# Attention scores as 64-row products on alternating halves of the array, in place of DMA-stacked 128-row products

## The chip, the cores and the metric

The kernel runs on one core of a Trainium2 chip. The metric is the device time of one execution in microseconds, the median of several runs. A profile is the record of one execution, taken by the hardware profiler; its times are counted from the first instruction (the span's start).

The names of the engines in the profile: PE is TensorE (matrix products), PEld the loading of its stationary operand, DVE is VectorE, ACT is ScalarE, POOL is GpSimd, and SP is SyncE, which here only issues DMA transfers.

## The reference, cut to what matters

A two-layer encoder over 512 tokens of width 1024: stick-breaking attention with 16 heads of 64, a squared-ReLU MLP of width 4096, a gated linear recurrence, a second MLP, and a final norm. All in float32. The part that the change touches is the score product `z` in

```python
z = jnp.einsum('bhqd,bhkd->bhqk', qb, kb).astype(jnp.float32) * scale   # per 128-query block
mask = k_pos < q_pos
log_keep = jnp.where(mask, jax.nn.log_sigmoid(-z), 0.0)
after = lax.cumsum(log_keep, axis=3, reverse=True) - log_keep
w = jnp.where(mask, jnp.exp(jax.nn.log_sigmoid(z) + after), 0.0)
outs.append(jnp.einsum('bhqk,bhkd->bhqd', w.astype(vb.dtype), vb))
```

Each head contracts over 64 numbers, and each block of 128 queries sees only the keys up to its own end.

## The kernel before, in words

**Precision.** A float32 matrix is split into a high part (rounded to the type fp32r, which PE takes in one pass) and a low part (the rest, again as fp32r). A product of two such matrices is the sum of three products: high by high, high by low, low by high. `three` (lines 234 to 236) does this for the dense layers.

**Attention.** Heads are worked in eight pairs, since two heads of 64 fill the 128 partitions of a tile. For each pair a dense product gives q (128 x 512, head 0 in partitions 0 to 63, head 1 in 64 to 127) and another gives k. ACT copies the product to the high part (line 349), DVE subtracts for the low part (line 350). Then `stacked` (line 341; line 368 for the first pair) issues DMA transfers on SP's queue that rebuild, for each head j, tiles of 128 partitions: `q{j}` holds q's high half above q's low half, `kh{j}` holds k's high half twice, `kl{j}` k's low half twice. That is twelve transfers of 64 x 512 numbers for a pair.

**Scores.** `score_steps` is a generator with eight steps a pair: head by head, and in each head the four query blocks. A step takes one PSUM bank of the tag `z` (there are two) and makes two products over all 128 rows: the stacked q block by `kh` (line 587) and by `kl` (line 588), with max(256, keys) columns, that is 256, 256, 384 and 512. Together they hold all four partial products, low by low too. What follows a step: two sigmoids on ACT (`w`, line 595, and `keep`, line 596, which read the bank; in the first pair DVE first copies the bank out, scaled, in line 593), a mask and a product on POOL (lines 600 and 610), and a scan on DVE (line 606).

**Values.** `value_steps` transposes the weights on PE (line 628), splits them on ACT and DVE, and multiplies by v (lines 654 and 655).

**What sets the order.** PE's order is written by hand: a loop runs over "fill" steps (the dense products of the next pairs' q and k in lines 234 to 236, of v in lines 503 to 505, and of the output projection), and between them it puts the score and value steps by due times: a pair's chain of `n` score steps starts at `SCORE0 + PACE * p` and is spread over `SCORES` = 19 fill steps; the value chain starts 23 fill steps later. The orders of ACT, DVE, POOL and SP are set by a scheduler from the program's dependences. SP's queue carries both the weight slabs (line 221) and the stacking transfers, in one order.

Of the kernel before, what the change touches and what calls it, by code (L numbers as in the profile page):

```python
# [11 lines left out]
F32 = mybir.dt.float32  # L12
BF16 = mybir.dt.bfloat16
F32R = mybir.dt.float32r
AF = mybir.ActivationFunctionType
ALU = mybir.AluOpType
PSUM = bass.MemoryType.PSUM

P = 128
S = 512  # L20
# [18 lines left out]
PACE = 23.7  # L39
SCORE0, SCORES = 12, 19  # L40
# [5 lines left out]
LATER = 1  # L46
# [14 lines left out]
EARLY = 5  # L61
# [3 lines left out]
def hybrid_encoder(  # L65
# [23 lines left out]
    nc = tc.nc  # L89
    V, A, G, PE = nc.vector, nc.scalar, nc.gpsimd, nc.tensor  # L90
# [10 lines left out]
    def bank(tag=None):  # L101
        if tag is None:
            tag = TAGS[turn[0] % len(TAGS)]
            turn[0] += 1
        return psum.tile([P, S], F32, tag=tag, name=f"ps_{tag}")

    def f(ap):
        return ap.bitcast(F32)
# [185 lines left out]
    NB = S // P  # L294
    PAIRS = H // 2
    half = [slice(0, HD), slice(HD, P)]
    so, early = {}, {}

    home = ctx.enter_context(tc.tile_pool(name="home", bufs=1))
    HOMES = (*(("keep", 4),) * 4, *(("w3", 3),) * 3, ("osum", 1))  # L300

    def home_tile(tag, n, name):
        return home.tile([P, S], F32, tag=tag, name=name, bufs=n)

    with ExitStack() as actx:
        hp = actx.enter_context(tc.tile_pool(name="hp", bufs=2))
# [3 lines left out]
        later = sp.tile([P, S], F32, tag="later", name="later")  # L310
# [3 lines left out]
            fill=1.0, base=0, channel_multiplier=1,  # L314
# [3 lines left out]
        for i in range(2):  # L318
            both = []
            for nm in ("h", "l"):  # L320
                t = sp.tile([P, 2 * P], F32R, tag=f"last{nm}{i}", name=f"last{nm}{i}")
# [4 lines left out]
        scans = []  # L326
        for i in range(3):
            sc = sp.tile([P, S + 1], F32, tag=f"scan{i}", name=f"scan{i}")
            G.memset(sc[:, S : S + 1], 1.0)
            scans.append(sc)  # L330

        q, kh, kl, v, w = {}, {}, {}, {}, {}
        norm = {}

        def stacked(tag, parts):

            both = []
            for j in range(2):
                t = hp.tile([P, S], F32R, tag=f"{tag}{j}", name=f"{tag}{j}")
                for a, part in zip(half, parts):  # L340
                    nc.sync.dma_start(out=f(t[a, :]), in_=f(part[half[j], :]))
                both.append(t)
            return both

        def parted(x, tag):

            xh = hp.tile([P, S], F32R, tag=f"{tag}h", name=f"{tag}h", bufs=1)
            xl = hp.tile([P, S], F32R, tag=f"{tag}l", name=f"{tag}l", bufs=1)
            A.copy(xh, x)
            V.tensor_tensor(xl, x, f(xh), ALU.subtract)  # L350
            return xh, xl

        def q_halves(pair, ps):
            q[pair] = stacked("q", parted(ps, "x"))

        def first_halves(pq, pk):

            qh, ql = parted(pq, "x")
            h = hp.tile([P, S], F32R, tag="th", name="th", bufs=3)
            l = hp.tile([P, S], F32R, tag="tl", name="tl", bufs=3)  # L360
            A.copy(h, pk)
            V.tensor_tensor(l, pk, f(h), ALU.subtract)
            q[0], kh[0], kl[0] = [], [], []
            for j in range(2):
                for tag, two, to in (("q", (qh, ql), q), ("kh", (h, h), kh), ("kl", (l, l), kl)):
                    t = hp.tile([P, S], F32R, tag=f"{tag}{j}", name=f"{tag}{j}")
                    for a, part in zip(half, two):
                        nc.sync.dma_start(out=f(t[a, :]), in_=f(part[half[j], :]))
                    to[0].append(t)

        def k_halves(pair, ps):
            ks = hp.tile([P, S], F32, tag="ks", name="ks", bufs=1)
            V.tensor_tensor(ks, ps, norm["r"], ALU.mult)
            h, l = parted(ks, "x")
            kh[pair] = stacked("kh", (h, h))
            kl[pair] = stacked("kl", (l, l))

        def xg_step(ps, k, wh, wl):
            three(ps, xgh[:, k, :], xgl[:, k, :], wh[:, k, :], wl[:, k, :], k == 0, k == C - 1)
# [20 lines left out]
        parts = [slab_parts(w_qk[i, 0], (0, 2, 4, 6, 8)) for i in range(2)]  # L400
# [162 lines left out]
        def late_slab(c, k0, tags):  # L563

            raw = wpool.tile([P, C, P], F32, tag="raw", name="raw", bufs=3)
            nc.sync.dma_start(out=raw[:, k0:, :], in_=w_so[c][:, k0:, :])
            n = (C - k0 + 3) // 4
            tiles = [hp.tile([P, S], F32R, tag=t, name=t) for t in tags]
            for i in range(n):
                a, b = k0 + 4 * i, min(k0 + 4 * i + 4, C)  # L570
                h, l = (t[:, : (b - a) * P].rearrange("p (k f) -> p k f", f=P) for t in tiles[i::n])
                A.copy(h, raw[:, a:b, :])
                V.tensor_tensor(l, raw[:, a:b, :], f(h), ALU.subtract)
            late[c] = Spread(tiles[:n], k0), Spread(tiles[n:], k0)

        late, marks = {}, {}
        turns = [0]

        def score_steps(pair):

            for j in range(2):
                for qb in range(NB):
                    n = (qb + 1) * P
                    nn = max(n, 2 * P)
                    lhsT = q[pair][j][:, qb * P : n]
                    z = bank("z")
                    PE.matmul(z[:, :nn], lhsT, kh[pair][j][:, :nn], start=True, stop=False)
                    PE.matmul(z[:, :nn], lhsT, kl[pair][j][:, :nn], start=False, stop=True)
                    keep = home_tile("keep", 4, "keep")
                    pool = home if qb == NB - 1 else hp  # L590
                    wt = pool.tile([P, n], F32, tag=f"w{qb}", name=f"w{qb}", bufs=3)
                    if pair == 0:
                        V.tensor_tensor(keep[:, :n], z[:, :n], norm["r"][:, :n], ALU.mult)
                        z = keep
                    A.activation(wt, z[:, :n], AF.Sigmoid, scale=norm["rp"][:, qb : qb + 1])
                    marks["keep"] = A.activation(  # L596
                        keep[:, :n], z[:, :n], AF.Sigmoid, scale=norm["rn"][:, qb : qb + 1]
                    )
                    t = wt[:, qb * P : n]
                    G.affine_select(  # L600
                        t, t, pattern=[[-1, P]], compare_op=ALU.is_gt,
                        fill=0.0, base=0, channel_multiplier=1,
                    )
                    sc = scans[turns[0] % 3]
                    turns[0] += 1
                    V.tensor_tensor_scan(  # L606
                        sc[:, S - n : S][:, ::-1], keep[:, :n][:, ::-1], later[:, S - n :][:, ::-1],
                        1.0, ALU.mult, ALU.max,
                    )
                    G.tensor_tensor(wt, wt, sc[:, S - n + 1 : S + 1], ALU.mult)  # L610
                    w[pair, j, qb] = wt
                    yield

        lows = []

# [68 lines left out]
        fill = []  # L684
# [28 lines left out]
        for p in range(PAIRS):  # L713
            less = LESS * (p == PAIRS - 1)
            chains += [
                [score_steps(p), 8, SCORE0 + PACE * p + LATER * (p == 0), SCORES - less - LATER * (p == 0)],
                [value_steps(p), 18, VAL0 + PACE * p + HOLD * (p == 0), VALS - less],
            ]
        inv = inverse()
# [6 lines left out]
        done = 0  # L726
        for i in range(AHEAD, n_fill):
            if i == LATE - 14:
                late_slab(4, EARLY, ("kh0", "kl0"))
                late_slab(5, EARLY, ("kh1", "kl1"))  # L730
            if i == LATE - 8:
                late_slab(6, 0, ("q0", "q1", "kh0", "kh1"))
            if i == LATE:
                x = [home_tile(tag, n, "x") for tag, n in HOMES[:7]]
                for c in range(7):
                    nc.sync.dma_start(out=x[c], in_=xT[:, c, :])
                for c in early:
                    G.tensor_tensor(x[c], x[c], early[c], ALU.add)
            next(steps)
            if i in (SUMS, BROAD):  # L740
                next(inv)
            if i == BROAD:
                with tc.issue_after(norm["copy"].ins):
                    q_halves(*held_halves.pop())
            if i == LATE // 2:
                soft.send(marks["keep"])
            while done < len(due) and due[done][0] < i + 1:
                next(chains[due[done][1]][0])
                done += 1
# [49 lines left out]
    class Mlp:  # L799
# [60 lines left out]
        def square(self, t):  # L860
            self.squares = self.A.activation(t, t, AF.Square)
# [585 lines left out]
    with ExitStack() as rctx:  # L1447
# [35 lines left out]
        ps, xc, aa, a0, om, z, gin, pg = ({} for _ in range(8))  # L1483
        r = None
# [31 lines left out]
        turns = count()  # L1516
# [128 lines left out]
        for k in range(C):  # L1645
            for c in range(4):
                ps, wh, wl = begun[c]
# [195 lines left out]
```

## Time and profile before

| | |
|---|---|
| median of 3 runs | 1028.99 us (1027.84 to 1029.25) |
| the profiled execution | 1029.37 us, span 1027.5 us |
| PE busy | 1019.4 us (99% of the span) |
| DVE, ACT, POOL busy | 857.0, 700.8, 171.1 us |
| score products (lines 587 and 588) | 64 each, first at 28.6 us, last at 205.0 us |
| stacking transfers (lines 341 and 368) | 96 of 128 KB, issued from about 21 to 183 us |

The span is 1.87 us shorter than the profiled execution's own time; sums are made against the latter. A PE record is longer than the time until the next product starts: products are pipelined, and the end of a record is modelled. So what a product costs PE is read from the distance of starts, not from its duration.

### The profile page before, as it was taken

Reading aid. Unit: us, or ns where it says so; the run is one execution under the profiler, and the core shown is the slowest. Engines: PE = TensorE matmul, PEld = TensorE weight load, DVE = VectorE, ACT = ScalarE, POOL = GpSimd, SP = SyncE. Lnnn points to the kernel's source line nnn. Section 1 sums busy time; section 2 is a strip of 40 time slices with the busy share of each in tenths; the row PEclk is TensorE's granted clock in tenths of the full one; section 3 lists DMA queues with packets and bytes.
Section 4 is the critical chain, followed back from the end, with each engine's and each line's share of the span. In section 5 each row is a group of like instructions: output and inputs, shape, how many; then the busy total and the mean of one; then the engine's idle time right before and its main releaser. Section 6 shows DMA issues by size and latency. Waiting matters only on the chain.

```text
span 1027.5 us, 15928 instructions
## 1 busy us (share of the span) xinstructions
PE 1019.4 (99%) x5890; PEld 892.0 (87%) x5890; DVE 857.0 (83%) x1149; ACT 700.8 (68%) x1084; POOL 171.1 (17%) x237
## 2 busy tenths in 40 slices
PE   9999999999999999999999999999999999999997
PEld 7888888888888988988988888888888988988986
DVE  7988787848789898898899888984689898898898
ACT  7777676836766773873875799964755774874866
POOL 0454344420010010010011121200010110010012
PEclk9999999999999999999999999999999999999999
DMA  7745354527537667667682575452436677667653
GB/s 235 222 121 146 120 149 102 160 95 291 136 77 197 170 154 197 172 145 201 176 209 80 152 184 157 103 205 90 97 81 185 166 162 191 166 157 195 170 116 115
DMA packets 53116, 160.46 MB, mean 156 GB/s; under 512 B 6704, under 2 KB 7984, under 8 KB 53040
## 3 DMA queue, kind: packets, MB, share of 16 engines
q1 hardware_dynamic: 41952, 120.21, 35.8%
q0 software_dynamic: 10656, 38.80, 22.9%
q8 instruction: 46, 0.75, 0.3%
q10 hardware_dynamic: 432, 0.44, 0.1%
q14 instruction: 30, 0.25, 0.1%
HBM read 137.41 MB, written 4.19 MB: 138 GB/s over the span
## 4 chain that ended last, share of the span: by engine, by line
PE 90%; DVE 4%; ACT 4%; issue 1%; DMA 1%; SPq 0%; POOL 0%; DVEq 0%; ACTq 0%; POOLq 0%
PE ps_t L1135 15%; PE ps_acc L1000 9%; PE ps_acc L1135 8%; PE ps_z L1000 6%; PE ps_acc L236 5%; PE ps_acc L235 5%; PE ps_acc L234 5%; PE ps_z L1135 4%; PE ps_o L1000 3%; PE ps_t L234 2%; PE ps_t L235 2%; PE ps_t L236 2%; PE ps_o L234 2%; PE ps_o L235 2%; PE ps_o L236 2%; PE ps_z L236 2%
## 5 line engine op out<-in xcount | busy, mean ns | idle before, releaser
L789 ACT CAST wh<-b 128x1024 fp32r<-128x1024 f32 x168 | 174.0, 1051 | 116.9 <-DVE b L789 71.8
L789 DVE TENSOR_TENSOR wl<-b,wh 128x1024 fp32r<-128x1024 f32 x168 | 203.1, 1220 | 37.8 <-ACT wh L789 36.6
L1076 POOL DMA_DIRECT2D b<-in_w_dn x40 | 34.9, 874 | 364.6 <-DVE b L789 268.4
L234 PE MATMUL ps_acc<-xgh,wh 128*128 128x512 f32 x192 | 78.6, 409 | 0.0
L236 PE MATMUL ps_acc<-xgl,wh 128*128 128x512 f32 x192 | 75.3, 392 | 0.0
L235 PE MATMUL ps_acc<-xgh,wl 128*128 128x512 f32 x192 | 75.2, 392 | 0.0
L229 DVE TENSOR_TENSOR wl<-raw,wh 128x512 fp32r<-128x512 f32 (+2 forms) x70 | 62.0, 913 | 15.4 <-ACT wh L227 15.3
L789 ACT ACTIVATE u<-u 128x512 f32<-128x512 f32 x100 | 63.2, 633 | 14.2 <-DVE u L789 12.6
L606 DVE TENSOR_TENSOR_SCAN scan<-keep,later 128x128 f32<-128x128 f32 (+1 forms) x64 | 58.4, 915 | 16.7 <-ACT keep L596 10.4
L227 ACT CAST wh<-raw 128x512 fp32r<-128x512 f32 (+2 forms) x70 | 50.7, 759 | 21.1 <-PE ps_acc L236 7.3
L610 POOL TENSOR_TENSOR w<-w,scan 128x128 f32<-128x128 f32 (+1 forms) x64 | 52.8, 826 | 56.0 <-DVE scan L606 51.3
L789 DVE TENSOR_TENSOR b<-b,b 128x1024 f32<-128x1024 f32 x48 | 58.7, 1223 | 1.2
L1076 POOL DMA_DIRECT2D b<-in_w_up x24 | 20.8, 868 | 231.0 <-DVE b L789 81.1
L789 DVE TENSOR_TENSOR u<-u 128x512 f32<-128x512 f32 (+1 forms) x92 | 54.9, 597 | 4.5 <-ACT u L789 2.5
L789 ACT CAST wh<-raw 128x1024 fp32r<-128x1024 f32 x46 | 48.1, 1048 | 2.5 <-PE ps_acc L1135 2.4
L1135 PE MATMUL ps_t<-wh,bh 128*128 128x512 f32 x120 | 47.0, 392 | 0.1
L1135 PE MATMUL ps_t<-wh,bl 128*128 128x512 f32 x120 | 46.9, 391 | 0.0
L789 DVE TENSOR_TENSOR sl<-u,sh 128x512 fp32r<-128x512 f32 (+2 forms) x50 | 37.5, 750 | 10.3 <-ACT sh L789 10.3
L1000 PE MATMUL ps_z<-xgh,wh 128*128 128x256 f32 x192 | 45.0, 278 | 0.2
L789 DVE TENSOR_TENSOR wl<-raw,wh 128x1024 fp32r<-128x1024 f32 x36 | 44.3, 1231 | 0.8 <-ACT wh L789 0.8
L1000 PE MATMUL ps_acc<-low,wh 128*128 128x256 f32 x192 | 44.7, 277 | 0.0
L789 DVE TENSOR_TENSOR bl<-u,bh 128x1024 fp32r<-128x1024 f32 (+2 forms) x26 | 33.9, 1304 | 12.4 <-ACT bh L789 12.3
(418 smaller groups left out, 3218.1 us busy)
## 6 DMA issues: line engine op xcount, KB each, us to landing
b<-in_w_dn SPq DMA_DIRECT2D x48, 512.0 KB, 4.5
b<-in_w_dn POOLq DMA_DIRECT2D x40, 512.0 KB, 5.8
b<-in_w_up SPq DMA_DIRECT2D x36, 512.0 KB, 4.8
b<-in_w_up POOLq DMA_DIRECT2D x24, 512.0 KB, 5.5
raw<-in_w_m SPq DMA_DIRECT2D x16, 512.0 KB, 4.0
raw<-in_w_dn SPq DMA_DIRECT2D x16, 512.0 KB, 4.6
raw<-in_w_in SPq DMA_DIRECT2D x16, 512.0 KB, 4.0
raw<-in_w_qk SPq DMA_DIRECT2D x12, 512.0 KB, 3.7
```

The source lines that it names most:

```text
L227: A.copy(wh[:, k, :], raw[:, k, :])
L229: V.tensor_tensor(wl[:, k, :], raw[:, k, :], f(wh[:, k, :]), ALU.subtract)
L234: PE.matmul(ps, wh, ah, start=start, stop=False)
L235: PE.matmul(ps, wl, ah, start=False, stop=False)
L236: PE.matmul(ps, wh, al, start=False, stop=stop)
L606: V.tensor_tensor_scan(sc[:, S - n : S][:, ::-1], keep[:, :n][:, ::-1], later[:, S - n :][:, ::-1], 1.0, ALU.mult, ALU.max,)
L610: G.tensor_tensor(wt, wt, sc[:, S - n + 1 : S + 1], ALU.mult)
L789: ins = getattr(self.e, name)(*args, **kwargs)
L1000: PE.matmul(ps[:, i * HS : (i + 1) * HS], m, y, start=new and i == k == low == 0 and y is h, stop=(low, i, k) == steps[-1], skip_group_che ...
L1076: G.dma_start(out=unit[b].rearrange("p j n -> p (j n)"), in_=unit["src"](to), accum_op=ALU.add)
L1135: PE.matmul(sums[to][i], a[:, j, block, i * P : (i + 1) * P], y[:, j, :], start=new and g == j == n == 0 and a is h, stop=g == j == 1 and ...
```

## The change

The stacking is left out. q and k stay as ACT and DVE write them: four tiles `qh`, `ql`, `kh`, `kl` of 128 partitions with the two heads of the pair one above the other. A head's product takes its 64 partitions of both operands. The score generator now has four steps a pair, one for each query block. A step takes both banks of the tag `z`, one for each head, and makes six products of 64 rows: high by high for head 0, for head 1, then q high by k low for both, then q low by k high for both. So consecutive products use different halves of the array's rows and different banks. The low-by-low product is no longer computed. The work after a product (`square`) is the same, for head 0 and then head 1. The due times get `NB` = 4 in place of 8 for the number of steps; the late weight slabs take the new tiles' buffers.

```diff
-        def stacked(tag, parts):
-            both = []
-            for j in range(2):
-                t = hp.tile([P, S], F32R, tag=f"{tag}{j}", name=f"{tag}{j}")
-                for a, part in zip(half, parts):
-                    nc.sync.dma_start(out=f(t[a, :]), in_=f(part[half[j], :]))
-                both.append(t)
-            return both
...
+        def parted(to, pair, tag, x):
+            h, l = (hp.tile([P, S], F32R, tag=f"{tag}{i}", name=f"{tag}{i}") for i in "hl")
+            A.copy(h, x)
+            V.tensor_tensor(l, x, f(h), ALU.subtract)
+            to[pair] = h, l
...
-            for j in range(2):
-                for qb in range(NB):
-                    lhsT = q[pair][j][:, qb * P : n]
-                    z = bank("z")
-                    PE.matmul(z[:, :nn], lhsT, kh[pair][j][:, :nn], start=True, stop=False)
-                    PE.matmul(z[:, :nn], lhsT, kl[pair][j][:, :nn], start=False, stop=True)
...
+            (qh, ql), (kh, kl) = q[pair], ks[pair]
+            for qb in range(NB):
+                n = (qb + 1) * P
+                nn = max(n, 2 * P)
+                zs = [bank("z") for _ in range(2)]
+                for i, (a, b) in enumerate(((qh, kh), (qh, kl), (ql, kh))):
+                    for z, rows in zip(zs, half):
+                        PE.matmul(
+                            z[:, :nn], a[rows, qb * P : n], b[rows, :nn], start=i == 0, stop=i == 2
+                        )
+                for j, z in enumerate(zs):
+                    square(j, qb, n, z)
+                yield
...
-                [score_steps(p), 8, SCORE0 + PACE * p + LATER * (p == 0), SCORES - less - LATER * (p == 0)],
+                [score_steps(p), NB, SCORE0 + PACE * p + LATER * (p == 0), SCORES - less - LATER * (p == 0)],
...
-                late_slab(4, EARLY, ("kh0", "kl0"))
-                late_slab(5, EARLY, ("kh1", "kl1"))
+                late_slab(4, EARLY, ("kh", "kl"))
+                late_slab(5, EARLY, ("kh", "kl"))
...
-                late_slab(6, 0, ("q0", "q1", "kh0", "kh1"))
+                late_slab(6, 0, ("qh", "qh", "ql", "ql"))
```

How this moves the instructions, at the two places of which the prediction speaks. First PE, from the second pair's scores on (names: `ps_z` the score bank, `ps_acc` the running dense product, `w_...` a weight tile that is transposed, `ident` the identity). Before, pair 1's third and fourth block of head 0:

```order
L587 MATMUL ps_z<-kh_736,q_849 128x384
L588 MATMUL ps_z<-kl_742,q_849 128x384
L628 MATMUL ps_t<-ident,w_799 128x128
L234 MATMUL ps_acc<-xgh,wh 128x512
L235 MATMUL ps_acc<-xgh,wl 128x512
L236 MATMUL ps_acc<-xgl,wh 128x512
```

and in the changed kernel, pair 1's first block of both heads:

```order
L236 MATMUL ps_acc<-xgl,wh 128x512
L590 MATMUL ps_z<-kh,qh 128x256 x2
L590 MATMUL ps_z<-kl,qh 128x256 x2
L590 MATMUL ps_z<-kh,ql 128x256 x2
L611 MATMUL ps_t<-ident,w_739 128x128
```

Two products of 128 rows in a step have become six of 64 rows (each row "x2" is one for each half), between neighbours of 128 rows; the steps are half as many.

Second DVE, in the first pair's scores (`keep` from `ps_z` is the copy that frees a bank, `scan_...` the scan's output, `v_...` a value tile). Before:

```order
L593 TENSOR_TENSOR keep<-ps_z,r 128x256
L606 SCALAR_TENSOR_TENSOR scan_118<-keep,later 128x128
L593 TENSOR_TENSOR keep<-ps_z,r 128x384
L350 TENSOR_TENSOR xl<-ks,xh 128x512
L606 SCALAR_TENSOR_TENSOR scan_120<-keep,later 128x256
L593 TENSOR_TENSOR keep<-ps_z,r 128x512
```

and in the changed kernel:

```order
L563 TENSOR_TENSOR keep<-ps_z,r 128x256 x2
L339 TENSOR_TENSOR kl<-ks,kh 128x512
L487 SCALAR_TENSOR_TENSOR v_505<-ps_acc,rc,v_505 128x4x64
L576 SCALAR_TENSOR_TENSOR scan_122<-keep,later 128x256
L576 SCALAR_TENSOR_TENSOR scan_118<-keep,later 128x256
L563 TENSOR_TENSOR keep<-ps_z,r 128x384 x2
```

The copies out of the banks now come in twos, and the third block's copies stand behind both scans of the second block.

More of the change, by code (lines that the diff above doesn't have):

```diff
@@ L330, in hybrid_encoder @@
             scans.append(sc)
-        q, kh, kl, v, w = {}, {}, {}, {}, {}
+        q, ks, v, w = {}, {}, {}, {}
         norm = {}
-        def stacked(tag, parts):
-            both = []
-            for j in range(2):
-                t = hp.tile([P, S], F32R, tag=f"{tag}{j}", name=f"{tag}{j}")
-                for a, part in zip(half, parts):
-                    nc.sync.dma_start(out=f(t[a, :]), in_=f(part[half[j], :]))
-                both.append(t)
-            return both
[L345 to L351, printed above, removed]
+        def parted(to, pair, tag, x):
[3 more added lines that the diff above has]
+            to[pair] = h, l
@@ L353, in q_halves @@
         def q_halves(pair, ps):
-            q[pair] = stacked("q", parted(ps, "x"))
+            parted(q, pair, "q", ps)
         def first_halves(pq, pk):
[L358 to L363, printed above, removed]
-            for j in range(2):
[L365 to L369, printed above, removed]
@@ L371, in k_halves @@
-        def k_halves(pair, ps):
[L372 to L376, printed above, removed]
+            parted(q, 0, "q", pq)
+            parted(ks, 0, "k", pk)
+        def k_halves(pair, ps):
+            t = hp.tile([P, S], F32, tag="ks", name="ks", bufs=1)
+            V.tensor_tensor(t, ps, norm["r"], ALU.mult)
+            parted(ks, pair, "k", t)
@@ L579, in score_steps @@
         def score_steps(pair):
-            for j in range(2):
-                for qb in range(NB):
-                    n = (qb + 1) * P
-                    nn = max(n, 2 * P)
-                    lhsT = q[pair][j][:, qb * P : n]
-                    z = bank("z")
[L587 to L612, printed above, removed]
@@ new lines, in square @@
+            def square(j, qb, n, z):
+                keep = home_tile("keep", 4, "keep")
+                pool = home if qb == NB - 1 else hp
+                wt = pool.tile([P, n], F32, tag=f"w{qb}", name=f"w{qb}", bufs=3)
+                if pair == 0:
+                    V.tensor_tensor(keep[:, :n], z[:, :n], norm["r"][:, :n], ALU.mult)
+                    z = keep
+                A.activation(wt, z[:, :n], AF.Sigmoid, scale=norm["rp"][:, qb : qb + 1])
+                marks["keep"] = A.activation(
+                    keep[:, :n], z[:, :n], AF.Sigmoid, scale=norm["rn"][:, qb : qb + 1]
+                )
+                t = wt[:, qb * P : n]
+                G.affine_select(
+                    t, t, pattern=[[-1, P]], compare_op=ALU.is_gt,
+                    fill=0.0, base=0, channel_multiplier=1,
+                )
+                sc = scans[turns[0] % 3]
+                turns[0] += 1
+                V.tensor_tensor_scan(
+                    sc[:, S - n : S][:, ::-1], keep[:, :n][:, ::-1], later[:, S - n :][:, ::-1],
+                    1.0, ALU.mult, ALU.max,
+                )
+                G.tensor_tensor(wt, wt, sc[:, S - n + 1 : S + 1], ALU.mult)
+                w[pair, j, qb] = wt
@@ new lines, in score_steps @@
+            (qh, ql), (kh, kl) = q[pair], ks[pair]
[7 more added lines that the diff above has]
+                            z[:, :nn], a[rows, qb * P : n], b[rows, :nn], start=i == 0, stop=i == 2
+                        )
+                for j, z in enumerate(zs):
+                    square(j, qb, n, z)
+                yield
```

## The prediction

> **What bounds the kernel now.** I read the page's totals and slices first, then the table of stages, then who PE waits for.
>
> ```profile
> PE 1019.4 (99%) x5890; PEld 892.0 (87%) x5890; DVE 857.0 (83%) x1149; ACT 700.8 (68%) x1084; POOL 171.1 (17%) x237
> ...
> PE   9999999999999999999999999999999999999997
> ...
> PEclk9999999999999999999999999999999999999999
> ...
> PE 90%; DVE 4%; ACT 4%; issue 1%; DMA 1%; SPq 0%; POOL 0%; DVEq 0%; ACTq 0%; POOLq 0%
> ...
> 25.00:50.00 25.00, 25.00 (x166) 22.53 (x165) 22.06 (x35) 18.78 (x39) 10.14 (x16) 1.00 0.78 225
> ...
> 100.00:125.00 25.00, 25.00 (x155) 22.09 (x154) 18.61 (x31) 16.51 (x38) 8.91 (x17) 1.00 0.38 106
> ...
> 500.00:1028.00 528.00, 520.95 (x2925) 453.39 (x2923) 448.61 (x559) 366.35 (x511) 61.29 (x66) 1.00 0.58 149
> ...
> PE ps_z L396 <- DVE dense_ones L118: 1.1, 1, 1.1
> ...
>   ACT keep L596: 0.4, 1
> ```
>
> PE is busy 99% of the span, at the full granted clock, and the chain that ended last is 90% PE. In the stage rows (PE, PEld, DVE, ACT, POOL, clock, DMA share) PE is busy for all 25 us of each attention stage and DVE at most for 22.06. The only listed wait of PE is 1.1 us at the start; the rows of line 587 add 0.4 us before one score product. So a microsecond of PE time saved or added in attention is a microsecond of the end, as long as no other engine takes the lead: DVE has 3 us of 25 to spare where it is fullest (25 to 50 us), more elsewhere, and after 500 us PE is again the fullest (520.95 of 528, DVE 448.61).
>
> What does a product cost PE? Not its record, but the distance from its start to the next. The timeline of PE, within the third pair:
>
> ```profile
> 75.92 0.33 PE L587 MATMUL ps_z<-kh,q 128*128 128x384 f32 x1
> 76.09 0.34 PE L588 MATMUL ps_z<-kl,q 128*128 128x384 f32 x1
> 76.26 0.27 PE L628 MATMUL ps_t<-ident,w 128*128 128x128 f32 x1
> ...
> 76.61 0.39 PE L235 MATMUL ps_acc<-xgh,wl 128*128 128x512 f32 x1
> ...
> 78.12 0.39 PE L587 MATMUL ps_z<-kh,q 128*128 128x512 f32 x1
> 78.34 0.39 PE L588 MATMUL ps_z<-kl,q 128*128 128x512 f32 x1
> 78.58 0.60 PE L628 MATMUL ps_t<-ident,w 128*128 128x128 f32 x4
> ...
> 79.25 0.39 PE L235 MATMUL ps_acc<-xgh,wl 128*128 128x512 f32 x1
> ...
> 80.64 0.28 PE L587 MATMUL ps_z<-kh,q 128*128 128x256 f32 x1
> 80.76 0.28 PE L588 MATMUL ps_z<-kl,q 128*128 128x256 f32 x1
> 80.88 0.40 PE L234 MATMUL ps_acc<-xgh,wh 128*128 128x512 f32 x1
> ```
>
> Two products of 256 columns take 80.88 - 80.64 = 0.24 us, two of 384 take 0.34, two of 512 take 0.46. A record of 0.39 outlasts its 0.23 of pitch by 0.16 us: the next product enters while the last one still leaves the array. Between 78.58 and 79.25 lie four transposes and one 512-column product (left out): (0.67 - 0.23) / 4 = 0.11 each, though a transpose has only 128 columns.
>
> **What the removal of the stacking is worth.** The rows of line 341:
>
> ```profile
> L341 SPq DMA_DIRECT2D kh<-xh x28: 461/587/965, 33.0 to 175.5; - x28
> ...
>   DVE xl L350: 1.2, 1
> ...
> DMA to landing us min/median/max: 2.2/2.4/6.6
> ```
>
> 96 transfers go, each some 0.59 us of SP's queue and 2.4 us to landing. The only listed waiter is DVE, 1.2 us once, for a buffer that a transfer still read; PE waits for none, since q and k are made a pair ahead. So I cost this part at nothing. The PE work of the pair before hides the landing now, and no cover is needed later, since the tiles are ready when DVE has written them. The weight slabs behind these transfers on SP's queue are issued earlier; PE waits for no slab, so this too is nothing. ACT and DVE keep their copies and subtractions.
>
> **What the products cost.** Before, a head's four blocks take 0.24 + 0.24 + 0.34 + 0.46 = 1.28 us, a pair 2.56, the eight pairs 20.5 us. Now each block has three products of the same columns for each head. No row shows a 64-row product, so the bounds come from those of 128 rows:
>
> - If the two halves run side by side, a block costs three pitches where it cost four: 20.5 x 3/4 = 15.4 us, **5.1 us less**.
> - If they run one after the other at the pitch of 128 rows, it is six for four: 30.7 us, **10.2 us more**.
>
> Between them lies the loading of the stationary operand:
>
> ```profile
> 22.22 0.95 PE L458 MATMUL ps_z<-ones,ssq 128*128 128x1 f32 x8
> ...
> 23.35 0.40 PE L235 MATMUL ps_t<-xgh,wl 128*128 128x512 f32 x1
> ...
> 118.30 0.19 PEld L587 LDWEIGHTS ps_z<-kh,q 128*128 128x128 f32 x1
> 118.41 0.19 PEld L588 LDWEIGHTS ps_z<-kl,q 128*128 128x128 f32 x1
> 118.53 0.19 PEld L234 LDWEIGHTS ps_acc<-xgh,wh 128*128 128x128 f32 x1
> ```
>
> Eight products of a single column, and one of 512 columns behind them (left out), take 23.35 - 22.22 = 1.13 us: (1.13 - 0.23) / 8 = 0.11 us each. That is the price of a load, whatever streams. If the loads of the two halves queue for one path, six products cost at least 0.66 us: 0.18 more than now in each 256-column block of a pair (0.48), 0.02 less in the 384 block (0.68), and 0.23 less in the 512 block, where three streams of 0.23 bind: 0.11 us a pair, **0.9 us more** in all.
>
> I take side by side. The two products of a couple share neither operand rows nor bank; and the loads in the rows last 0.19 us and start 0.11 apart, and the products' records overlap by 0.16 us, so the array already holds several instructions in different phases. That is an argument from the nearest rows, not a measurement.
>
> The Trainium skill, page "TensorE: Matmul & The Clock Gate", section "Part 3: Packing small matmuls — row/col tiling", says that products in different row groups run concurrently, and gives 3.07 times for four of 32 rows; by it the term is the 5.1 us saved. No run here shows it yet.
>
> **The borders.** 32 blocks lie between products of 128 rows: 64 changes of shape. What does one cost? The nearest row is the transpose, also another kind of product between dense ones: from 76.26 to 76.61 a transpose and a 512-column product (left out) take 0.35, of which 0.11 + 0.23 are their own, so its two borders cost 0.01 us together, 64 borders 0.3 us. The upper end: if the array must run empty at each border, the 0.16 us by which a record outlasts its pitch is lost 64 times, 10.2 us. I take twice the transpose's price, 0.6 us, because a transpose uses all rows too.
>
> **The banks.** A step now needs both `z` banks free at once.
>
> ```profile
> L593 DVE TENSOR_TENSOR keep<-ps_z,r x8: 277/470/691, 29.9 to 44.0; 128x128 f32<-128x128 f32 x2, 128x256 f32<-128x256 f32 x2, 128x384 f32<-128x384 f32 x2, 128x512 f32<-128x512 f32 x2
> ...
> L596 ACT ACTIVATE keep<-ps_z,rn x52: 352/524/722, 48.2 to 197.2; 128x128 f32<-128x128 f32 x13, 128x256 f32<-128x256 f32 x13, 128x384 f32<-128x384 f32 x13, 128x512 f32<-128x512 f32 x13
> ...
>   PE ps_z L588: 16.6, 21
> ```
>
> From the second pair on a block's second bank is free after four sigmoids of at most 0.72 us, some 2.9 us; four steps are spread over 19 fill steps, each at least three 512-column products or six of 256 (0.69 us), so 4.75 x 0.69 = 3.3 us lie between blocks, and score and value products come on top. ACT waits for the product in 21 cases (the last row, of line 595), so it takes it up at once. In the first pair DVE frees the banks in twos, and the third block's copies stand behind both scans of the second on the engine's fullest stage; behind them wait the value copies of v, and behind those PE's `acc` banks. In the last pair the steps are 3.75 fill steps apart. I put 0.5 us for both; 0 to 2 us are possible.
>
> **The sum**, against the profiled execution: 1029.4 - 5.1 + 0.6 + 0.5 = 1025.4 us. That execution is 0.4 above the median, so 1025.0 as a median.
>
> **The rivals.**
>
> *The array runs empty at the borders.* Place: between each block of 64-row products and its neighbours. For it: loads and products run ahead of one another only within one shape in all rows here. Against it: the transposes' 0.01 us. Price up to 0.16 us for each of 64 borders; it eats the gain from (5.1 - 0.5) / 64 = 0.07 us on. At the full price 1029.0 - 5.1 + 10.2 + 0.5 = 1034.6 us, slower. Beside it: the Trainium skill, "TensorEngine Tiling (Array Packing)", section "Key Properties", says that a change of tiling mode drains TensorE. The transposes' rows show no such loss, but they don't leave the 128-row mode.
>
> *Loads queue.* Side by side in the streams, but 0.11 us for each load: 1029.0 + 0.9 + 0.6 + 0.5 = 1031.0 us. For it: the one-column products, which nothing but loading can hold at 0.11. Against it: the overlapping load records.
>
> *The change doesn't do what it says.* The halves follow one another: 1029.0 + 10.2 + 0.6 + 0.5 = 1040.3 us. For it: every pair of starts in the trace is a full pitch apart. Against it: all of those use all rows, so they could not be closer.
>
> **How the numbers follow.** Forecast 0.46, borders 0.2, loads 0.17, one after the other 0.12, anything else (a stall at the banks) 0.05. What a measurement of this kernel can tell from no change is about 0.2%, 2 us. The forecast is faster with nearly all of its chance (0.44), the borders at a low price add 0.02: faster 0.46. Same: borders near 0.07 us (0.08), loads that cost little (0.09), bank stalls (0.02): 0.19. Slower: the rest, 0.35. The range's lower end is the forecast without borders and stalls, 1029.0 - 5.1 = 1023.9, and a little below it, 1023; the upper end takes in the loads with half the borders' price and the borders at full price, 1038; above it lies most of the fourth case. The forecast's own range is 1023 to 1027.
>
> **What the changed profile would show.** Right: starts of the two halves of a couple almost at one time and couples 0.12 to 0.23 us apart; no gap wider than 0.02 at the borders; PE's waits near 1.5 us in all. Borders: the first 64-row product, or the first 128-row one behind, comes 0.1 us or more late. Loads: products of 256 columns 0.11 apart one by one, those of 512 couples 0.23. One after the other: 0.23 between all starts at 512 columns. The prediction is wrong as well if PE idles for `ps_z` by more than 2 us.

## The result, and the profile after

The changed kernel takes 1039.32 us in the median (1038.95 to 1039.58, 4 runs) against 1029.12 us (1027.84 to 1029.66, 4 runs) of the kernel before: a ratio of 1.0101, 95% interval 1.0083 to 1.0118. It is **slower by 10.2 us**. The forecast was 1025.0 us, faster, with a range to 1038; both were missed.

The page of the changed kernel, its totals and the DMA queue of SP, then the stage row from 125 to 150 us (PE, PEld, DVE, ACT, POOL, clock, DMA share):

```profile
PE 1026.4 (99%) x5954; PEld 886.0 (85%) x5954; DVE 852.7 (82%) x1149; ACT 699.6 (67%) x1084; POOL 181.0 (17%) x237
...
q1 hardware_dynamic: 34272, 107.63, 30.5%
...
125.00:150.00 25.00, 24.03 (x154) 19.65 (x152) 19.29 (x31) 16.96 (x36) 11.12 (x14) 1.00 0.19 61
```

The 12.6 MB of stacking are gone from the queue (107.63 MB where there were 120.21), and the balance below needs no term for it. PE has 64 more products and now stands idle in attention, for about 1 us of these 25. The last value product of attention starts at 239.8 us where it started at 229.0; from there to the end both kernels take nearly the same time (0.7 us less now).

One block of two heads in the timeline of PE of the changed kernel (the fourth pair's second block), between a value product and a dense product of 512 columns:

```profile
102.59 0.39 PE L638 MATMUL ps_o<-tl,v 128*128 128x512 f32 x1
102.91 0.39 PE L590 MATMUL ps_z<-kh,qh 64*128 64x256 f32 x2
103.13 0.28 PE L590 MATMUL ps_z<-kl,qh 64*128 64x256 f32 x2
103.25 0.28 PE L590 MATMUL ps_z<-kh,ql 64*128 64x256 f32 x2
103.46 0.50 PE L234 MATMUL ps_acc<-xgh,wh 128*128 128x512 f32 x1
103.80 0.40 PE L235 MATMUL ps_acc<-xgh,wl 128*128 128x512 f32 x1
```

Each row "x2" is one product of either half. They start together: the row of two lasts 0.28 us, no longer than the record of one product. From couple to couple it is 103.25 - 103.13 = 0.12 us, one pitch of 256 columns. So **the halves run side by side**, as forecast. But four distances are too long:

| from, to | distance | its own pitch | lost |
|---|---|---|---|
| last 128-row product, first couple | 0.32 | 0.23 | 0.09 |
| first couple, second couple | 0.22 | 0.12 | 0.10 |
| last couple, first 128-row product | 0.21 | 0.12 | 0.09 |
| first 128-row product, the next | 0.34 | 0.23 | 0.11 |

Why each border loses twice is seen in the rows of the weight loads (PEld) in the same place:

```profile
102.37 0.19 PEld L638 LDWEIGHTS ps_o<-tl,v 128*128 128x128 f32 x1
102.91 0.19 PEld L590 LDWEIGHTS ps_z<-kh,qh 64*128 64x128 f32 x2 [0.35 <-issue]
103.02 0.19 PEld L590 LDWEIGHTS ps_z<-kl,qh 64*128 64x128 f32 x2
103.14 0.19 PEld L590 LDWEIGHTS ps_z<-kh,ql 64*128 64x128 f32 x2
103.45 0.19 PEld L234 LDWEIGHTS ps_acc<-xgh,wh 128*128 128x128 f32 x1
103.56 0.19 PEld L235 LDWEIGHTS ps_acc<-xgh,wl 128*128 128x128 f32 x1
```

Inside one shape a load starts when the product before it starts (103.14 for the product at 103.25), and is hidden. At a border it starts only with its own product, at 102.91 and 103.45: first the array runs empty (0.09 us behind the last stream), then the load lies open, which means that no product streams beside it (0.11 us), and only then does the product stream. That this product streams late is seen in its record, 0.50 where its neighbours have 0.40, and in the next start. The loads of the two halves go side by side too ("x2" at one time).

By the medians of all 32 blocks a block loses 0.093 + 0.105 + 0.091 + 0.103 = 0.39 us, so 0.196 us for each border and **12.5 us** for the 64. That is the main loss. A second one is in the table of PE's waits:

```profile
PE ps_o L638 <- DVE lastl L627: 2.0, 5, 1.0
...
PE ps_o L638 <- DVE tl L627: 1.0, 1, 1.0
```

By the distances of starts these six waits come to 4.0 us, against 0.3 us at one value product before: 3.7 us more. The balance: -5.1 (couples) + 12.5 (borders) + 3.7 (waits) = 11.1 us. The last value product moved by 10.8 us and the end by 10.2. Two terms of some 0.5 us are not in it and go against each other: the pairs of products in the kernel before stood 0.5 us further apart, all in all, than their pitches; and the product behind each of the six waits is about 0.1 us late once more (144.37 in the rows below). So 0.3 us stay open.

What the wait is: the timeline of DVE before (two rows of this stretch), then in the changed kernel, then PE at the same place.

```profile
136.60 0.27 DVE L644 TENSOR_TENSOR lastl<-ps_t,lasth 128x128 fp32r<-128x128 f32 x1
...
138.25 1.23 DVE L606 TENSOR_TENSOR_SCAN scan<-keep,later 128x512 f32<-128x512 f32 x1 [0.90 <-ACT keep L596]
```

```profile
141.52 2.39 DVE L576 TENSOR_TENSOR_SCAN scan<-keep,later 128x512 f32<-128x512 f32 x2 [0.91 <-ACT keep L566]
143.83 0.26 DVE L627 TENSOR_TENSOR lastl<-ps_t,lasth 128x128 fp32r<-128x128 f32 x1
```

```profile
142.89 0.29 PE L637 MATMUL ps_o<-lasth,v 128*128 128x256 f32 x1
144.15 0.39 PE L638 MATMUL ps_o<-lastl,v 128*128 128x256 f32 x1 [0.97 <-DVE lastl L627]
144.37 0.28 PE L479 MATMUL ps_acc<-wh,xgh 128*128 128x256 f32 x1
```

A small piece of the value chain (0.26 us) stands on DVE behind the two scans of the fourth block, which now come one after the other and themselves wait for four sigmoids in a row. Before, it stood ahead of a single scan. PE stands still for 144.15 - 142.89 - 0.12 = 1.1 us, and the next product is another 144.37 - 144.15 - 0.12 = 0.1 us late, as at a border. Five of the six waits are of this kind; at the sixth (219.42 us) a subtraction for a late weight slab, 1.38 us, stands between the scans and the piece as well.

### The profile page after: what moved, and what is told of

Its sections match the earlier page's. It is cut to its first block, busy times and chain, and to the rows that moved or that the text cites. A ratio compares the mean times of both kernels' runs of the same rounds, so it can differ in the third digit from the quotient of the medians.

```text
span 1037.6 us, 15819 instructions
## 1 busy us (share of the span) xinstructions
PE 1026.4 (99%) x5954; PEld 886.0 (85%) x5954; DVE 852.7 (82%) x1149; ACT 699.6 (67%) x1084; POOL 181.0 (17%) x237
## 3 DMA queue, kind: packets, MB, share of 16 engines
q1 hardware_dynamic: 34272, 107.63, 30.5%
## 4 chain that ended last, share of the span: by engine, by line
PE 93%; DVE 3%; ACT 2%; issue 1%; DMA 0%; DVEq 0%; ACTq 0%
PE ps_t L1118 16%; PE ps_acc L983 9%; PE ps_acc L1118 8%; PE ps_z L983 7%; PE ps_acc L234 5%; PE ps_acc L236 5%; PE ps_acc L235 5%; PE ps_o L983 4%; PE ps_z L1118 4%; PE ps_t L234 2%; PE ps_t L235 2%; PE ps_t L236 2%; PE ps_z L590 2%; PE ps_o L234 2%; PE ps_o L236 2%; PE ps_o L235 2%
## 5 line engine op out<-in xcount | busy, mean ns | idle before, releaser
L772 ACT ACTIVATE u<-u 128x512 f32<-128x512 f32 x100 | 63.2, 633 | 14.2 <-DVE u L772 12.6
L576 DVE TENSOR_TENSOR_SCAN scan<-keep,later 128x128 f32<-128x128 f32 (+3 forms) x64 | 51.6, 822 | 21.4 <-ACT keep L566 18.0
L580 POOL TENSOR_TENSOR w<-w,scan 128x128 f32<-128x128 f32 (+3 forms) x64 | 63.0, 1002 | 12.5 <-DVE scan L576 11.0
L570 POOL TENSOR_SCALAR_AFFINE_SELECT w<-w 128x128 f32<-128x128 f32 x64 | 29.5, 463 | 112.4 <-ACT w L565 112.0
```

Of the source, the lines that this page charges most:

```text
L570: G.affine_select(t, t, pattern=[[-1, P]], compare_op=ALU.is_gt, fill=0.0, base=0, channel_multiplier=1,)
L576: V.tensor_tensor_scan(sc[:, S - n : S][:, ::-1], keep[:, :n][:, ::-1], later[:, S - n :][:, ::-1], 1.0, ALU.mult, ALU.max,)
L772: ins = getattr(self.e, name)(*args, **kwargs)
```

## The experiments

Times beside each are medians, and ratios are to the kernel before on the same chip (1029.2 to 1029.7 us there).

**The border alone.** The kernel before, its second product on 64 rows:

```diff
-  PE.matmul(z[:, :nn], lhsT, kl[pair][j][:, :nn], start=False, stop=True)
+  PE.matmul(z[:, :nn], q[pair][j][:HD, qb * P : n], kl[pair][j][:HD, :nn], start=False, stop=True)
```

> The kernel before, with one edit: the second score product (by k's low half) takes only the upper 64 rows, so the low-by-low product is left out and every step holds one 64-row product between products of 128 rows. Streams, order, transfers and banks stay as before; 64 steps make 128 borders. Theory of the borders (0.09 us for the array to run empty and 0.11 us for a stationary load that can't be fetched ahead, 0.20 us each, as the changed kernel's starts show): 128 x 0.20 = 25.6 us more, 1054.7 us. As the prediction's rival priced it (0.16 us each, the records' tail): 20.5 us more, 1049.6. Rival, the loss of the change is that 64-row products follow one another at a full pitch and shape changes are free: a product of 64 rows replaces one of 128 at the same pitch, no change, 1029 us.

Measured 1052.51 us, ratio 1.0221 (1.0204 to 1.0238): 22.9 us more. In its timeline of PE:

```profile
49.77 0.28 PE L587 MATMUL ps_z<-kh,q 128*128 128x256 f32 x1
49.98 0.38 PE L588 MATMUL ps_z<-kl,q 64*128 64x256 f32 x1
50.29 0.50 PE L234 MATMUL ps_acc<-xgh,wh 128*128 128x512 f32 x1
50.63 0.40 PE L235 MATMUL ps_acc<-xgh,wl 128*128 128x512 f32 x1
```

The same four losses around a single product: 49.98 - 49.77 - 0.12 = 0.09; 50.29 - 49.98 - 0.12 = 0.19 (its open load and the array running empty behind it); 50.63 - 50.29 - 0.23 = 0.11. They sum to 0.39, 25 us in 64 steps. Between the first dense product and the last value product this kernel takes 23.5 us more (23.8 with the 0.3 us of wait that the kernel before had at a value product, and this one has not); some 1 us I can't place. So borders alone, with order, banks and transfers unchanged, cost more than the whole change did. The rival (64-row products are simply slow, shapes may change for nothing) is out.

**Heads apart.** The changed kernel, two loops exchanged:

```diff
-  for i, (a, b) in enumerate(((qh, kh), (qh, kl), (ql, kh))):
-      for z, rows in zip(zs, half):
+  for z, rows in zip(zs, half):
+      for i, (a, b) in enumerate(((qh, kh), (qh, kl), (ql, kh))):
```

> The changed kernel with one edit: a block's six products are issued head by head (three of the upper half, then three of the lower) and no longer in turns. Borders, banks and work are the same. If the halves run side by side in the changed kernel: a half's three products must follow one another, and only the first of the second head can run beside the last of the first, so a block costs five pitches where it cost three: 2 x 0.64 us in a pair for each head's worth of blocks, 8 pairs: 10.2 us more, 1049.5 us; if nothing overlaps at the change of heads, six pitches, 15.3 us more, 1054.6 us. Rival, the halves follow one another already: no change, 1039.3 us.

Measured 1039.86 us, ratio 1.0098 (1.0083 to 1.0113): as the changed kernel. By the expectation that would have spoken for halves that follow one another. The timeline of PE says otherwise. The program has, in this order,

```
L590 MATMUL ps_z<-kh,qh 128x256
L590 MATMUL ps_z<-kl,qh 128x256
L590 MATMUL ps_z<-kh,ql 128x256
L590 MATMUL ps_z<-kh,qh 128x256
L590 MATMUL ps_z<-kl,qh 128x256
L590 MATMUL ps_z<-kh,ql 128x256
```

and PE did

```profile
98.20 0.39 PE L590 MATMUL ps_z<-kh,qh 64*128 64x256 f32 x2
98.42 0.29 PE L590 MATMUL ps_z<-kl,qh 64*128 64x256 f32 x2
98.54 0.29 PE L590 MATMUL ps_z<-kh,ql 64*128 64x256 f32 x2
98.76 0.55 PE L611 MATMUL ps_t<-ident,w 128*128 128x128 f32 x3
```

The rows don't name the half, but a block has only two products `kh,qh`, the first and the fourth of the program, and both stand in the row that starts at 98.20, 0.01 us apart. So head 1's first started beside head 0's first, ahead of the second and third. The time says the same: in the program's order a block would take five pitches, and the kernel some 10 us more. The alternation in the change is not what makes the halves run side by side; PE does it. My expectation held each half to the program's order, and that was wrong, so this run did not test what it was made for.

**One half.** So I gave PE no second half: all six products from the upper 64 rows (head 1's scores are left out, its bank holds head 0's once more).

```diff
-  for z, rows in zip(zs, half):
+  for z, rows in zip(zs, half[:1] * 2):
```

> The changed kernel with all six products of a block taken from the upper 64 rows: head 1's scores are left out, and its bank is filled with head 0's products once more. Instructions, borders, banks and order are the same. In the run with the heads apart the trace showed that PE starts the other half's product 0.01 us after the first even where three products of one half stand ahead of it; here there is no other half. Theory (in the changed kernel the halves run side by side): six pitches where there were three, 15.3 us more, 1054.6 us. Rival (the halves never ran side by side, and the starts in the trace only look so): no change, 1039.3 us.

Measured 1053.41 us, ratio 1.0234 (1.0218 to 1.0250): 14.1 us more than the changed kernel.

```profile
49.51 0.50 PE L590 MATMUL ps_z<-kh,qh 64*128 64x256 f32 x2
49.85 0.39 PE L590 MATMUL ps_z<-kl,qh 64*128 64x256 f32 x2
50.09 0.39 PE L590 MATMUL ps_z<-kh,ql 64*128 64x256 f32 x2
50.41 0.50 PE L234 MATMUL ps_acc<-xgh,wh 128*128 128x512 f32 x1
```

The six products take 50.41 - 49.51 = 0.90 us; in the changed kernel 103.46 - 102.91 = 0.55. The difference, 0.35, is three pitches of 256 columns. So the halves do run side by side in the changed kernel, and the gain of the couples is real. That 14.1 and not 15.3 came out fits the value products, which by their starts wait 1.5 us less here.

**Stacked products, in twos.** The changed kernel's steps with the products and transfers of before:

```diff
   zs = [bank("z") for _ in range(2)]
-  for i, (a, b) in enumerate(((qh, kh), (qh, kl), (ql, kh))):
-      for z, rows in zip(zs, half):
-          PE.matmul(z[:, :nn], a[rows, qb * P : n], b[rows, :nn], start=i == 0, stop=i == 2)
+  for j, z in enumerate(zs):
+      lhsT = q[pair][j][:, qb * P : n]
+      PE.matmul(z[:, :nn], lhsT, kh[pair][j][:, :nn], start=True, stop=False)
+      PE.matmul(z[:, :nn], lhsT, kl[pair][j][:, :nn], start=False, stop=True)
```

> The changed kernel's four steps a pair with both banks taken at once, but the products and the stacking transfers of the kernel before (four products of 128 rows in a step). No border. If the order of the work alone (sigmoids, scans and POOL products in twos) causes the waits of the value products that the changed kernel's trace shows (six gaps, 4.0 us, 3.7 more than before): 3.7 us more than before, 1032.8 us. Rival, the whole loss of the change lies in the order and the banks: 1039 us. Rival, the waits come from the borders, which delay the scores: 1029 us.

Measured 1037.02 us (1036.10 to 1038.50), ratio 1.0073 (1.0058 to 1.0088): 7.4 us more than before, without one border. PE's waits:

```profile
PE ps_t L633 <- DVE tl L649: 1.6, 1, 1.6
PE ps_o L660 <- DVE tl L649: 1.2, 1, 1.2
...
PE ps_o L660 <- DVE lastl L649: 1.0, 2, 0.7
PE ps_z L614 <- DMA kl<-tl: 0.8, 1, 0.8
```

So the order in twos costs by itself, and twice the 3.7 us that were expected. By its time alone the run is nearer to the rival that puts the whole loss down to order and banks (1039 us); what speaks against that rival is the 0.39 us at each block in the changed kernel's starts and the run with the border alone. Nor is it the 3.7 us of the changed kernel one for one: 0.8 us is a wait for a stacking transfer, which the changed kernel does not have (the first step needs both heads' tiles at once), and the waits stand at other lines. The direction holds (scores in twos hold up the value chain on DVE), the size does not carry over, and the 3.7 us of the changed kernel rest on its own trace.

**Scores earlier, scores later.** The changed kernel with the score chain over 16 fill steps, then over 21, where it was 19.

```diff
-SCORE0, SCORES = 12, 19
+SCORE0, SCORES = 12, 16
```

```diff
-SCORE0, SCORES = 12, 19
+SCORE0, SCORES = 12, 21
```

> The changed kernel with the score chain spread over 16 fill steps where it was 19, so that a pair's last block comes some 2 fill steps (2 us) earlier. In the changed kernel the value products' waits end with DVE's low half of the last transposed block, which stands behind two scans of 512 columns on DVE; those would start earlier and be over in time. Theory: most of the 3.7 us goes, 1035.6 to 1036.5 us, and PE idles less before the value products. Rival, the loss is all in the products and borders: no change, 1039.3 us.

> The changed kernel with the score chain spread over 21 fill steps where it was 19. Moving it the other way (16) made the kernel slower: the two 512-column scans in a row held DVE, which works in order, at other places, and the waits of the value products grew. With 21 the order on DVE puts the low half of the last transposed block ahead of the two 512-column scans. Theory (the waits come from scans in twos ahead of the value chain's small pieces): the six waits of 4.0 us mostly go, 1036 to 1037 us; the borders stay at 12.7 us. Rival (any place of a couple of 512 columns blocks something of the value chain as long): waits of 4 us at other lines, 1039 us.

Measured 1042.26 us with 16 (ratio 1.0121, 1.0106 to 1.0136) and 1039.07 us with 21 (1.0094, 1.0076 to 1.0112): 2.9 us slower than the changed kernel, and no difference. Both expectations of a gain failed. DVE with 16, and POOL at the same time:

```profile
139.21 2.39 DVE L576 TENSOR_TENSOR_SCAN scan<-keep,later 128x512 f32<-128x512 f32 x2 [1.64 <-ACT keep L566]
141.53 0.39 DVE L627 TENSOR_TENSOR tl<-ps_t,th 128x256 fp32r<-128x256 f32 x1
...
142.44 2.17 DVE L229 TENSOR_TENSOR wl<-raw,wh 128x512 fp32r<-128x512 f32 x2
144.54 0.28 DVE L627 TENSOR_TENSOR lastl<-ps_t,lasth 128x128 fp32r<-128x128 f32 x1
```

```profile
140.59 3.48 POOL L580 TENSOR_TENSOR w<-w,scan 128x512 f32<-128x512 f32 x2
```

The scans come 2 us earlier, but DVE then stands idle for 1.64 us in front of them with the value chain's pieces queued behind, and after them two subtractions for a weight slab take 2.17 us together beside POOL's two products of 512 columns (in the changed kernel two of them took 1.28 us from 139.34 us on, while POOL stood idle), so `lastl` is late again. With 21 the waits moved to other pieces:

```profile
PE ps_t L611 <- DVE tl L627: 1.3, 2, 1.1
...
PE ps_o L638 <- DVE lastl L627: 0.7, 1, 0.7
```

By the starts the waits come to 3.2 us where they were 4.0, and the time is the same. So the rival of that run (waits as long at other lines, wherever the couples of 512 columns come) fits best. Its cause is only in part shown: at the longest of these waits (at 102 us) slab subtractions stand between the couple and the late piece. That no other place is better, these runs do not show.

**Three runs a pair.** The changed kernel with the first and second block in one run, the second in columns 256 to 511 of the same banks:

```diff
-  for qb in range(NB):
+  for qbs in ((0, 1), (2,), (3,)):
       zs = [bank("z") for _ in range(2)]
+      for at, qb in enumerate(qbs):
...
-  [score_steps(p), NB, ...
+  [score_steps(p), 3, ...
```

> The changed kernel with the first and second block of a pair in one run of twelve 64-row products: the second block uses columns 256 to 511 of the same two banks. Three runs a pair where there were four, so 48 borders where there were 64. Work, couples and banks are the same. Theory of the borders (0.18 to 0.20 us each): 16 x 0.2 = 3.2 us less, 1036.2 us, if the waits of the value products stay as they are; these may move by 1 to 2 us either way, so the sum of gaps at the borders in the trace (12.7 us in the changed kernel) is the sharper figure: 9.5 us expected. Rival, the loss goes with the number of 64-row products or with the banks, not with the borders: no change in the sum, 1039.3 us or more.

Measured 1033.67 us, ratio 1.0043 (1.0028 to 1.0058): 5.7 us less than the changed kernel. By the distances of starts a run loses 0.39 us as before, 24 x 0.39 = 9.4 us in all, close to the 9.5 expected: 3.1 us less. The rest are waits: PE's list has

```profile
PE ps_o L642 <- DVE tl L631: 0.6, 1, 0.6
PE ps_t L615 <- DVE tl L631: 0.4, 1, 0.4
```

and by starts they are 1.3 us where they were 4.0: 2.7 us less. 3.1 + 2.7 = 5.8, against the 5.7 measured. The number of 64-row products is the same as in the changed kernel, so the loss goes with the borders.

**What counts as a border.** The kernel of the border alone, with 96 rows in place of 64:

```diff
-  PE.matmul(z[:, :nn], q[pair][j][:HD, qb * P : n], kl[pair][j][:HD, :nn], start=False, stop=True)
+  PE.matmul(z[:, :nn], q[pair][j][:96, qb * P : n], kl[pair][j][:96, :nn], start=False, stop=True)
```

> The kernel before with the second score product on the upper 96 rows of both operands (in the run with the border alone it was 64 rows, 23 us more). A third of the low-by-low product is left in, half of it out. If any change in the number of rows makes a border, the array empties and the load waits as with 64 rows: 23 us more, 1052.5 us. If only products that fit in half the array make one, and 96 rows still count as the whole array: no change, 1029.5 us, and no gap of 0.09 or 0.11 us at these products. No theory of this case says which; it tells what the border is a border of.

Measured 1029.75 us, ratio 1.0005 (0.9995 to 1.0015): no difference. Its timeline of PE:

```profile
53.75 0.39 PE L587 MATMUL ps_z<-kh,q 128*128 128x512 f32 x1
53.98 0.40 PE L588 MATMUL ps_z<-kl,q 96*128 96x512 f32 x1
54.22 0.40 PE L234 MATMUL ps_acc<-xgh,wh 128*128 128x512 f32 x1
```

All distances are 0.23 to 0.24. So fewer rows alone are no border: 96 rows make none, 64 rows do. No run here tells where between them it begins.

No version here beats the kernel before. One that did would need few runs: the couples save 5.1 us and a border costs 0.196, so it breaks even at 26 borders, 13 runs for 32 blocks, if nothing waits. With two banks of 512 columns a pair needs at least three runs, 24 in all. A single block can't pay: the widest saves one pitch, 0.23 us, and pays 0.39.

## Why the prediction was wrong, step by step

- **PE bounds the stage, and the end follows it**: right. The last value product came 10.8 us later, the end 10.1 (by the two profiled spans).
- **The stacking costs nothing**: it held. 12.6 MB of transfers went, and the balance closes to 0.3 us without a term for it; no run tests it alone.
- **Side by side, 5.1 us less**: right. Couples of 256 columns are 0.12 us apart, the loads of the halves run beside one another, and one half alone made the kernel 14.1 us slower. The rivals of queueing loads and of halves one after the other are out, though the latter's 1040.3 us was nearest to the measured time: by the time alone it would have been taken for the cause.
- **The borders, 0.6 us**: this is the step that failed. They measured 12.5 us. I priced a border by the transposes, the nearest other kind of product in the trace. But a transpose has 128 rows like its neighbours, and the runs with 96 and with 64 rows in the same place show that the number of rows is what counts. I had that doubt in the prediction, and doubling the price did not answer it. The upper bound was too low as well: I took the tail of a record (0.16 us) and forgot the stationary load. At a border the load isn't fetched ahead, so 0.09 us of emptying and 0.11 us of loading add up to 0.20, over the 0.07 at which the change breaks even. The load's price, 0.11 us, stood in the prediction; what I did not ask is when it is hidden, namely when it starts with the product before it.
- **The rival of the array that runs empty** had the right place and half of the mechanism, at a price of 10.2 us where 12.5 were measured. The Trainium skill, "TensorEngine Tiling (Array Packing)", section "Key Properties", has the rule that a change of tiling mode drains TensorE; the trace agrees, with 0.09 us for the drain and as much again for the load. I gave this rival a chance of 0.2, against a row that did not bear on it.
- **The banks, 0.5 us**: this term was mis-sized as well. The products of line 590 never waited for a bank: the only row that names the sigmoid which frees one is 0.4 us, once, of the weight loads, and they stand idle as long at a border without it (0.35 us at 102.91). But taking both heads at once made DVE's order lumpy, and PE waited 3.7 us longer for the value chain. I looked at who waits for the bank and not at what stands behind the work that the bank feeds, two scans of 512 columns in a row.
- The range's upper end, 1038, fell 1.3 us short: to the full price of the borders I had added neither the open load nor the waits for the value chain.

## What to carry to other kernels

Half-array products pay by the run and not by the product: a run of 64-row products between whole-array ones cost 0.39 us here, so it has to save more than that, 1.7 pitches of 512 columns, before it gains. Put all half-array work of a stage together, or fill the rows (with 96 of 128 there was no border here). And when two chains are taken in step for the sake of one engine, read what stands behind their lumps on the engines that work in order.

## What the runs showed that I had not expected

- A stationary load at a border isn't hidden: 0.11 us on top of the emptying, each time. The same 0.1 us stands behind each of PE's six waits for the value chain, where no shape changes.
- The two halves are fed apart from one another. With three products of the upper half ahead of the lower half's first in the program, PE started the latter beside the first of them (both at 98.20 us). The Trainium skill, "TensorE: Matmul & The Clock Gate", section "Part 3: Packing small matmuls — row/col tiling", says that products start and end in program order; between the halves the run with the heads apart shows otherwise.
- 96 rows cost no border: distances of 0.23 to 0.24 us, 1.0005 times the time before.
